# A row gradient through one DMA queue: loads and stores in threes, or in strict turn

## The chip, the cores and the metric

The kernel runs on one core of a Trainium2 chip. The metric is the device time of one execution in microseconds (us). Before the change four runs took 1247.53 to 1249.38 us, median 1249.04 us.

## What is computed

The input `x` is 8192 x 8192, float32. The output is its gradient along each row:

```
def reference(x: np.ndarray) -> np.ndarray:
    return np.gradient(x, axis=1)
```

Inside a row that is `(x[c+1] - x[c-1]) / 2`; in the first column it is `x[1] - x[0]`, in the last `x[m-1] - x[m-2]`. Every element is read once and written once: 268.44 MB in and 268.44 MB out.

## The kernel before

The 8192 rows are cut into `nsets` = 32 sets of 256 rows. Each of the 128 partitions holds R = 2 neighbouring rows of a set, so a set is 128 x 16384 float32, 8.39 MB, and a partition's part of it is one run of 65,536 bytes in memory. There are NB = 3 slots in the on-chip memory; set i lives in slot i % 3. A slot is 64 columns (SH) wider than a set: a load (L61) puts the set at column 64, and the result is written 64 columns to the left of its input in the same slot, so that a store (L97) takes columns 0 and up.

For each set there are four steps:

- L73, on POOL (GpSimd): the four end differences of each partition (two rows, two ends) go into a small tile `ends`. It waits for the set's load.
- L84, on DVE (VectorE): one custom instruction writes half the difference of the right and the left neighbour for all inner columns. It waits for L73. In the last set it is split into one instruction for each of the two rows.
- L95, a small copy that places the ends in the result, on POOL for sets with i % 5 in (1, 3), on DVE otherwise. It waits for L84.
- L97, the store, issued from SP (SyncE). It waits for L95. The last set has two stores of 4.19 MB, one for each row.

All DMAs are issued by SP, in program order, into one hardware queue (q1 in the profile). SP waits for the semaphores of a DMA before it issues it, and what comes later in SP's program waits behind. `manual_schedule` keeps the order as written, and the helper `chain` (L46 to L57) cuts each step's waits down to the ones named: a load of set i >= 3 waits only for the store of set i - 3, which frees its slot. What decides the order of the queue is where `load` is called: three loads before the loop (L67, L68), and at the end of every third turn of the loop three more (L102 to L104). With L for a load, S for a store and the set's number behind it, SP's order is

```
few L0 L1 L2 | S0 S1 S2 | L3 L4 L5 | S3 S4 S5 | L6 L7 L8 | ... | S27 S28 S29 | L30 L31 | S30 S31a S31b
```

where `few` is a load of 1 KB at L66 and S31a, S31b are the two stores of the last set.

Of the kernel before, what the change touches and what calls it, by code (L numbers as in the profile page):

```python
# [1 line left out]

# [4 lines left out]


@with_exitstack
def kernel(  # L10
    ctx: ExitStack,
    tc: tile.TileContext,
    x: bass.AP,
    out: bass.AP,
):

    nc = tc.nc
    P = nc.NUM_PARTITIONS
    n, m = x.shape
    R = 2
    NB = 3  # L30
    SH = 64  # L31
    W = R * m
    nsets = n // (P * R)
    f32 = x.dtype

    x_sets = x.rearrange("(s p t) m -> s p (t m)", p=P, t=R)
    out_sets = out.rearrange("(s p t) m -> s p (t m)", p=P, t=R)

    pool = ctx.enter_context(tc.tile_pool(name="pool", bufs=1))
    slots = [pool.tile([P, SH + W], f32, name=f"slot{k}", tag=f"slot{k}") for k in range(NB)]  # L40
    ends = pool.tile([P, nsets, R, 2], f32, name="ends", tag="ends")
    few = pool.tile([16, 16], f32, name="few", tag="few")
    loads, stores = [], [None] * nsets
    in_front = {}

    def chain(i, ins, *needed):  # L46

        group, engine = f"slot{i % NB}", ins.ins.engine  # L50
        keep = [o.ins for o in needed]
        if in_front.get(engine, (None,))[0] == group:
            keep.append(in_front[engine][1])
        tc.declare_no_dep(ins.ins, group=group, keep=keep, reason="implied by the needed step")
        tc.add_to_no_dep_group(group, ins.ins)
        in_front[engine] = group, ins.ins
        return ins  # L57

    def load(i):
        b = slots[i % NB]  # L60
        ins = nc.sync.dma_start(out=b[:, SH : SH + W], in_=x_sets[i])  # L61
        loads.append(chain(i, ins, *([stores[i - NB]] if i >= NB else [])))

    with tc.manual_schedule():

        nc.sync.dma_start(out=few[:], in_=x[0:16, 0:16])  # L66
        for i in range(NB):  # L67
            load(i)  # L68
        for i in range(nsets):
            b = slots[i % NB]  # L70
            xin = b[:, SH : SH + W].rearrange("p (t m) -> p t m", m=m)

            ins = nc.gpsimd.tensor_sub(  # L73
                out=ends[:, i, :, :],
                in0=xin[:, :, 1 : m : m - 2],
                in1=xin[:, :, 0 : m - 1 : m - 2],
            )
            at = [chain(i, ins, loads[i])]
            last = i == nsets - 1
            nr = 1 if last else R  # L80
            for r in range(0, R, nr):
                c0, c1 = r * m + 1, (r + nr) * m - 1

                ins = nc.vector._custom_dve(  # L84
                    dve_ops.TENSOR_TENSOR_REDUCE_SUB_MAX,
                    out=b[:, c0:c1],
                    in0=b[:, SH + c0 + 1 : SH + c1 + 1],
                    in1=b[:, SH + c0 - 1 : SH + c1 - 1],
                    s0=0.0,
                    s1=0.5,  # L90
                )
                halved = chain(i, ins, *at)
                res = b[:, r * m : (r + nr) * m].rearrange("p (t m) -> p t m", m=m)
                placer = nc.gpsimd if i % 5 in (1, 3) and not last else nc.vector
                ins = placer.tensor_copy(out=res[:, :, 0 : m : m - 1], in_=ends[:, i, r : r + nr, :])  # L95
                placed = chain(i, ins, halved)
                ins = nc.sync.dma_start(  # L97
                    out=out_sets[i, :, r * m : (r + nr) * m], in_=b[:, r * m : (r + nr) * m]
                )
                stores[i] = chain(i, ins, placed)  # L100
                at = [halved]
            if i % NB == NB - 1:  # L102
                for k in range(i + 1, min(i + 1 + NB, nsets)):
                    load(k)  # L104


# [1 line left out]
_INS = ['x']  # L108
_OUTS = [((8192, 8192), 'float32')]


# [23 lines left out]
```

## Time and profile before

| what | value |
|---|---|
| median of four runs | 1249.04 us |
| time of the profiled execution | 1249.38 us |
| its span, first to last instruction | 1247.4 us |
| moved | 536.88 MB, mean 430 GB/s over the span |
| DVE busy | 554.8 us (44%) |
| POOL busy | 8.9 us (1%) |
| DVE, one set (L84, 128 x 16382) | 17.22 us, 31 times |
| DVE, one row of the last set (128 x 8190) | 8.69 us, twice |
| L73 on POOL | 0.20 us, 32 times |
| L95 on DVE or POOL | 0.17 us or 0.19 us |
| load, issue to landing, median | 58.0 us |
| store, issue to landing, median | 40.4 us |

The profile of one execution gives, for each engine, its busy time; in 40 equal slices of the span the busy share of the 16 DMA engines and the GB/s that they moved; and for each group of DMA issues the time from issue to landing, which holds the time spent queued behind others. The timeline lists instructions in order of time, with the idle time of the engine ahead of them and what ended it in brackets: a POOL L73 that was released by `DMA slot<-in_x_dram` starts about 0.1 us after its load has landed, so the starts of the 32 L73 instructions are the landing times of the 32 loads. In SP's own timeline issues that follow each other are merged into one line (`x3`), with the time from the first to the last.

### The profile page before, as it was taken

Reading aid. Unit: us, or ns where it says so; the run is one execution under the profiler, and the core shown is the slowest. Engines: PE = TensorE matmul, PEld = TensorE weight load, DVE = VectorE, ACT = ScalarE, POOL = GpSimd, SP = SyncE. Lnnn points to the kernel's source line nnn. Section 1 sums busy time; section 2 is a strip of 40 time slices with the busy share of each in tenths; the row PEclk is TensorE's granted clock in tenths of the full one; section 3 lists DMA queues with packets and bytes.
Section 4 is the critical chain, followed back from the end, with each engine's and each line's share of the span. In section 5 each row is a group of like instructions: output and inputs, shape, how many; then the busy total and the mean of one; then the engine's idle time right before and its main releaser. Section 6 shows DMA issues by size and latency. Waiting matters only on the chain.

```text
span 1247.4 us, 243 instructions
## 1 busy us (share of the span) xinstructions
DVE 554.8 (44%) x54; POOL 8.9 (1%) x48
## 2 busy tenths in 40 slices
DVE  2850483069009702850582079009603840591083
POOL 0000000000000000000000000000000000000000
DMA  9999999999999999999999999999999999999989
GB/s 404 431 425 422 437 437 435 435 437 429 431 427 433 435 437 435 437 437 433 437 422 431 429 437 435 437 435 437 437 435 425 433 431 431 437 435 437 435 380 404
DMA packets 9394, 536.88 MB, mean 430 GB/s; under 512 B 1073, under 2 KB 1073, under 8 KB 1073
## 3 DMA queue, kind: packets, MB, share of 16 engines
q1 hardware_dynamic: 9392, 536.88, 99.6%
q14 instruction: 2, 0.01, 0.0%
HBM read 268.44 MB, written 268.44 MB: 430 GB/s over the span
## 4 chain that ended last, share of the span: by engine, by line
another core or an unknown queue 74%; DVE 18%; DMA 3%; issue 2%; POOL 1%; SPq 0%; POOLq 0%
DVE slot L84 18%; DMA slot<-in_x_dram 3%; POOL ends L73 0%; POOL slot L95 0%; SPq L61 0%; SPq L66 0%; DVE slot L95 0%; POOLq L130 0%
## 5 line engine op out<-in xcount | busy, mean ns | idle before, releaser
L84 DVE CUSTOM_DVE_ANT_0 slot<-slot 128x16382 f32<-128x16382 f32 (+1 forms) x33 | 551.3, 16706 | 670.2 <-POOL ends L73 670.2
L73 POOL TENSOR_TENSOR ends<-slot 128x4 f32<-128x4 f32 x32 | 6.4, 200 | 991.1 <-DMA slot<-in_x_dram 991.1
L95 DVE COPY slot<-ends 128x4 f32<-128x4 f32 (+1 forms) x21 | 3.6, 172 | 0.7
L95 POOL COPY slot<-ends 128x4 f32<-128x4 f32 x12 | 2.3, 191 | 207.9 <-DVE slot L84 207.9
L119 POOL MEMSET const-bfloat16-1.0<- 128x1 bf16 x1 | 0.1, 102 | 0.0
L119 POOL MEMSET const-uint8-127<- 128x1 uint8 x1 | 0.1, 102 | 0.0
L119 POOL MEMSET const-float32-0.0<- 128x1 f32 x1 | 0.1, 99 | 0.2 <-issue 0.2
L119 POOL MEMSET const-float32-1.0<- 128x1 f32 x1 | 0.1, 99 | 0.0
## 6 DMA issues: line engine op xcount, KB each, us to landing
out_dram<-slot SPq DMA_DIRECT2D x2, 4096.0 KB, 20.2
slot<-in_x_dram SPq DMA_DIRECT2D x32, 58.0
out_dram<-slot SPq DMA_DIRECT2D x31, 40.4
few<-in_x_dram SPq DMA_DIRECT2D x1, 1.0 KB, 1.4
```

Source lines behind the costliest of these rows:

```text
L73: ins = nc.gpsimd.tensor_sub(out=ends[:, i, :, :], in0=xin[:, :, 1 : m : m - 2], in1=xin[:, :, 0 : m - 1 : m - 2],)
L84: ins = nc.vector._custom_dve(dve_ops.TENSOR_TENSOR_REDUCE_SUB_MAX, out=b[:, c0:c1], in0=b[:, SH + c0 + 1 : SH + c1 + 1], in1=b[:, SH + c0 ...
L95: ins = placer.tensor_copy(out=res[:, :, 0 : m : m - 1], in_=ends[:, i, r : r + nr, :])
L119: nc = _bacc.Bacc("TRN2", target_bir_lowering=False, num_devices=1)
```

## The change

The loads are no longer called three at a time at the end of every third turn. From turn 1 to turn 29 each turn ends with one load, that of set i + 2. An empty line higher up goes as well.

```
@@ -99,9 +98,8 @@
                 )
                 stores[i] = chain(i, ins, placed)
                 at = [halved]
-            if i % NB == NB - 1:
-                for k in range(i + 1, min(i + 1 + NB, nsets)):
-                    load(k)
+            if 1 <= i < nsets - 2:
+                load(i + 2)
```

SP's order becomes

```
few L0 L1 L2 | S0 S1 | L3 S2 | L4 S3 | L5 S4 | L6 S5 | ... | L30 S29 | L31 S30 S31a S31b
```

The DMAs, their sizes, the slots, the arithmetic and each step's waits are the same; only the place of the loads L3 to L31 in SP's program differs. A load of set i + 2 still waits for the store of set i - 1.

## The prediction

> **What bounds the kernel now.** I read the page first: the slices and the DMA queue.
>
> ```profile
> DMA  9999999999999999999999999999999999999989
> GB/s 404 431 425 422 437 437 435 435 437 429 431 427 433 435 437 435 437 437 433 437 422 431 429 437 435 437 435 437 437 435 425 433 431 431 437 435 437 435 380 404
> q1 hardware_dynamic: 9392, 536.88, 99.6%
> L84 DVE CUSTOM_DVE_ANT_0 slot<-slot 128x16382 f32<-128x16382 f32 (+1 forms) x33 | 551.3, 16706 | 670.2 <-POOL ends L73 670.2
> ```
>
> The 16 DMA engines are busy from end to end (99.6% of the span) and DVE is idle for more than half of it. The transfers are the bound, and the only thing to win or lose is the rate at which they run. That rate has a ceiling of 437 GB/s that many slices touch and none passes; others lie at 422 to 433.
>
> Second, the timeline of POOL. Each L73 starts when its load has landed, so these starts are landing times:
>
> ```profile
> 140.69 0.20 POOL L73 TENSOR_TENSOR ends<-slot 128x4 f32<-128x4 f32 x1 [77.24 <-DMA slot<-in_x_dram]
> 160.02 0.20 POOL L73 TENSOR_TENSOR ends<-slot 128x4 f32<-128x4 f32 x1 [1.62 <-DMA slot<-in_x_dram]
> 180.11 0.20 POOL L73 TENSOR_TENSOR ends<-slot 128x4 f32<-128x4 f32 x1 [19.89 <-DMA slot<-in_x_dram]
> 257.60 0.20 POOL L73 TENSOR_TENSOR ends<-slot 128x4 f32<-128x4 f32 x1 [77.29 <-DMA slot<-in_x_dram]
> ```
>
> L4 lands 19.33 us after L3, L5 lands 20.09 us after L4. The next triples give 19.36 and 19.88, 19.34 and 19.75, 19.36 and 20.30. So the second load of a triple costs 19.33 us, which is the plain price of 8.39 MB (434 GB/s), and the third, the one with a store behind it, costs up to 1 us more. Over the ten triples the third load's surplus is 1.36 (L2), 0.76, 0.55, 0.42, 0.97, 0.01, 0.22, 0.00, 0.27, 0.28 us.
>
> Third, windows of 2.4 us around the end of L5 show where inside the load the surplus lies:
>
> ```profile
> 169.60:172.00 2.40, 2.40 (x1) 0.00 (x0) 1.00 1.01 437
> 172.00:174.40 2.40, 2.40 (x1) 0.00 (x0) 1.00 1.01 437
> 174.40:176.80 2.40, 2.40 (x1) 0.00 (x0) 1.00 1.27 437
> 176.80:179.20 2.40, 0.85 (x2) 0.00 (x0) 1.00 0.89 382
> 179.20:181.60 2.40, 1.26 (x1) 0.20 (x1) 1.00 1.01 437
> ```
>
> (The last number is GB/s, the one ahead of it the DMA share.) The rate is 437 until the last packets of L5 and 437 again with S3; it dips to 382 just at the switch from load to store. S3 had been in the queue since 158.43 and no engine ran dry, so this is no gap in the supply. At the end of L2 the same view gives 191 GB/s in one window of 2.4 us.
>
> Last, a whole cycle of three stores and three loads, from one first load to the next, lasts 116.91, 116.56, 116.41, 116.93, 116.37, 116.19, 115.92, 116.23, 116.30 us (L3 to L30), mean 116.42. Six plain transfers are 6 x 19.32 = 115.92. So one pair of switches, store to load and load to store, costs **0.50 us** on average, from 0.00 to 1.01; of that the third loads explain 3.48 / 9 = 0.39 and the other switch and rounding 0.11. In the last five cycles the mean is 0.28, in the first four 0.78.
>
> **The change part by part.** Removed and added in bytes, DMAs or instructions: nothing. Moved: 29 loads in SP's program, each with one DMA.
>
> *Does the queue run dry?* I lay the new order out with 19.32 us a transfer and 17.8 us from a landing to the store's issue (0.1 to start, L73 0.20, L84 17.22, L95 0.17 or 0.19, some 0.1 between). L2 lands at 63.2. S0 (issued at 40.88) runs to 82.5, S1 (issued at 60.30) to 101.8. L3 waits for S0: issued at 82.6, as now, runs 101.8 to 121.2. S2 is ready at 80.9 and now stands behind L3 in SP's program, so it is issued at about 83.0, 2 us later than it could be; it is not wanted until 121.2. L4 waits for S1 (101.8), runs 140.5 to 159.8. S3 is ready at 121.2 + 17.8 = 139.0 and is wanted at 159.8. L5 waits for S2 (140.5) and is wanted at 179.1. S4 is ready at 159.8 + 17.8 = 177.6 and wanted at 198.5. From there it repeats: a load is in the queue 38.6 us, a store 20.8 us before its turn, one or two transfers stand behind the running one, and SP's wait for a slot holds up no store that is needed. The compute of one set per 38.6 us stays hidden. Cost 0; if this cover were gone, each store would come with a hole (priced below).
>
> *The end.* Now S30 is issued at 1206.20, and L31 lands at 1207.8: the queue runs down, and the window 1203 to 1206 moves 66 GB/s. From L31's landing two plain transfers are 38.6, which gives 1246.4 of 1247.4: at most 1.0 us can come from that hole, and nothing if the slowest DMA engine finished L31 as S30 arrived. In the new order S30 is ready 20.8 us early. Bounds -1.0 to 0; I take 0, since the three windows around show some engines idle while others still moved L31, and the slowest decides.
>
> *The switches.* After L2, before has nine full pairs plus the switch into L30, whose other side is the run-down end. The new order has 29 pairs (S1-L3-S2 up to S29-L31-S30). The first switch, L2 to S0, is the same in both. No row shows loads and stores in strict turn, so the price of such a pair is bounded by the pairs here: 0.00 (the cycle of 115.92) and 1.01 (that of 116.93). With 4.54 us of surplus in before's nine pairs:
>
> - mean price 0.50: 29 x 0.50 - 4.54 = +10.0 us
> - first four as in before (3.13), then 25 at the late mean of 0.28 = 7.0: 10.1 - 4.54 = +5.6 us
> - at the ends: 0.00 gives -4.5, 1.01 gives +24.8
>
> The surplus shrinks in later cycles, which favours the second, but the late rows scatter (0.45, 0.27, 0.00, 0.31, 0.38) and do not go to nothing. Also the trace's DMA packet records show that by then the last engine ends a transfer over 4 us after the first, and it is the late engines that lose, because they still load while the others already store; with three times as many switches that lag has more occasions. I take the middle, 0.42 a pair: 29 x 0.42 - 4.54 = **+7.6 us**. Against the profiled execution 1249.38 + 7.6 = **1257.0 us**. That execution is 0.3 us over the median of 1249.04.
>
> A rule that would make it far worse: the Trainium skill, "DMA: Bandwidth & Descriptors", section "Anatomy of one DMA — SWDGE (gpsimd) path", puts a fixed cost of about 2.0 us on each DMA, mostly the receipt of the last write. Were that paid at every switch from load to store, 20 more of them would be 40 us by that page's figure, an estimate of 1289. The rows speak against it: 19.33 us between two landings leaves no 2 us, and a pair costs 0 to 1.01. The same page ("Two DMAs through the same engine are not ordered") says that an engine's reading and writing sides are separate and pipelined, which could let a store's reads run beside a load's writes and make switches a gain; no landing here is under 19.33 us apart, so nothing of the kind shows.
>
> **The rivals.**
>
> *Switches cost (forecast).* For: eight of ten third loads are longer than plain (by 0.22 us or more), no second load is, and the dip lies at the switch. Against: the price varies from 0 to 1.36 with no visible reason. 0.27 to 0.65 a pair: 1253 to 1264, centre 1257.
>
> *It is the third load, not the switch (faster).* The surplus could belong to three loads in a row with three stores piled up behind them, the deepest the queue gets. With one or two transfers waiting, as laid out above, the surplus would go: 1249.38 - 4.5 = 1244.8, or 1243.8 with the hole at the end. It decides from a price under 0.07 a pair (29 x 0.07 - 4.5 = -2.5). For it: cycles with 0.00 exist. Against: L2 had only S0 and just then S1 behind it, and paid the most, 1.36.
>
> *Cheap switches (same).* The engines drift apart and stop hindering each other, 0.07 to 0.24 a pair: 1247 to 1252.
>
> *Mixed traffic feeds on itself (much slower).* The lag between DMA engines grows until loads and stores always run side by side; at the early price of 0.78, 29 x 0.78 - 4.54 = +18 us, 1267; at 1.01, 1274. For it: the 191 GB/s window. Against: the trend falls.
>
> *The queue runs dry.* If my margins are wrong by a whole transfer, each set has a hole like that of 1203 to 1206, about 3 x (1 - 66/437) = 2.5 us, 29 times: 1322. The margins of 20.8 us speak against it.
>
> **How the numbers follow.** Forecast 0.60, faster 0.12, same 0.15, much slower 0.11, dry 0.02. A measurement of this kernel tells 0.2% (2.5 us) from no change, so faster is 0.12, same 0.15, slower 0.73. The range leaves out the faster case below 1247 and the part of the slow cases above 1268, some 0.20 in all: 1247 to 1268. The forecast's own range is 1253 to 1264.
>
> **What would show it.** Right: loads landing every 38.6 to 39.2 us, mean about 39.06 (2 x 19.32 + 0.42); slices mostly under 435 GB/s and none over 437; dips at the ends of loads; no window near 66 GB/s; SP issuing each store some 20 us before the load ahead of it lands. Wrong: landings every 38.64 us, or a mean rate over 430 GB/s (the third-load rival); landings over 41 us apart with idle windows (dry queue); a transfer faster than 19.32 us, which would mean that reads and writes help each other.

## The result, and the profile after

The changed kernel takes **1250.57 us** (median, 1249.10 to 1252.26), the kernel before 1248.90 us beside it: a ratio of 1.0015, 95% interval 1.001 to 1.002. I had forecast 1257.0. The direction holds, the size is a quarter of it: 1.7 us instead of 7.6, the place where my rival of cheap switches stood (1247 to 1252).

The page of the kernel after, its rate in 40 slices and its queue:

```profile
GB/s 403 436 430 411 434 436 436 434 422 436 434 432 432 422 436 430 434 436 434 434 436 424 436 436 432 434 432 426 434 436 435 432 436 432 434 434 436 436 434 342
q1 hardware_dynamic: 9392, 536.88, 99.6%
```

The queue is as full as before (99.6%) and the ceiling as high. Most low slices lie among the first 22; from the 23rd to the 39th all but one (426) are at 432 to 436. New is the last slice: 342 GB/s, where the kernel before had 404. Some DMA engines are done there while others still move data.

The timeline of POOL, the landing times of L2 to L7 and of the last three loads:

```profile
62.85 0.20 POOL L72 TENSOR_TENSOR ends<-slot 128x4 f32<-128x4 f32 x1 [2.64 <-DMA slot<-in_x_dram]
121.25 0.20 POOL L72 TENSOR_TENSOR ends<-slot 128x4 f32<-128x4 f32 x1 [58.21 <-DMA slot<-in_x_dram]
160.06 0.20 POOL L72 TENSOR_TENSOR ends<-slot 128x4 f32<-128x4 f32 x1 [21.09 <-DMA slot<-in_x_dram]
199.34 0.20 POOL L72 TENSOR_TENSOR ends<-slot 128x4 f32<-128x4 f32 x1 [39.08 <-DMA slot<-in_x_dram]
238.84 0.20 POOL L72 TENSOR_TENSOR ends<-slot 128x4 f32<-128x4 f32 x1 [39.30 <-DMA slot<-in_x_dram]
278.91 0.20 POOL L72 TENSOR_TENSOR ends<-slot 128x4 f32<-128x4 f32 x1 [22.36 <-DMA slot<-in_x_dram]
...
1132.38 0.20 POOL L72 TENSOR_TENSOR ends<-slot 128x4 f32<-128x4 f32 x1 [20.95 <-DMA slot<-in_x_dram]
1170.99 0.20 POOL L72 TENSOR_TENSOR ends<-slot 128x4 f32<-128x4 f32 x1 [38.41 <-DMA slot<-in_x_dram]
1209.65 0.20 POOL L72 TENSOR_TENSOR ends<-slot 128x4 f32<-128x4 f32 x1 [38.46 <-DMA slot<-in_x_dram]
```

From L3 on a landing follows the last by two transfers and one pair of switches; plain is 2 x 19.32 = 38.64. Early the differences are 38.81, 39.28, 39.50, 40.07 us; at the end 38.61 and 38.66. Summed: from L2 to L12 (21 transfers, 10 pairs) the surplus over plain is 4.87 us, from L12 to L22 (20, 10 pairs) it is 2.03, from L22 to L31 (18, 9 pairs) it is 0.02. So a pair costs 0.49, then 0.20, then **0.00 us**. That is nearly the whole difference from my sum: 29 pairs were to cost 29 x 0.42 = 12.2 us and cost 6.92. The early price is near the 0.42 that I had put on all of them, and it did not last. (Another 0.3 us lies at L2, whose switch I had taken to be the same in both kernels: L2 takes 20.35 us here and 20.69 before.)

Windows show it too, the first around the switch from L2 to S0, the second around the end of L27 (the last number is GB/s).

```profile
57.40:59.80 2.40, 2.40 (x1) 0.00 (x0) 1.00 1.42 437
59.80:62.20 2.40, 0.15 (x1) 0.19 (x1) 1.00 0.51 218
```

```profile
1051.80:1054.20 2.40, 0.00 (x0) 0.00 (x0) 1.00 1.01 437
1054.20:1056.60 2.40, 1.27 (x1) 0.20 (x1) 1.00 1.01 437
```

The first switch takes the rate down to 218 GB/s; the late one cannot be seen. In the trace's DMA packet records each engine carries a load as eight packets of 65,536 bytes, and a plain packet takes 2.42 us. The last packet of L2 took 3.15 to 3.70 us on all 16 engines: the surplus lies in the last packets ahead of the store.

What goes with it is in the same records, which give the end of each transfer on each of the 16 DMA engines. Worked out from them, the lag of each engine behind a schedule of 19.32 us a transfer (19.318 before rounding), in us, sorted (zero is the first engine at the end of L1):

```
after, L1    0.0  0.1  0.2  0.2  0.2  0.2  0.2  0.2  0.2  0.3  0.3  0.3  0.3  0.4  0.5  0.5
after, L7    1.8  2.0  2.1  2.1  2.1  2.2  2.5  2.5  2.9  3.1  3.1  3.2  3.3  3.5  3.6  5.1
after, L12   2.2  2.3  2.3  2.3  2.3  2.4  2.6  2.6  3.2  4.2  4.2  4.2  4.6  4.8  4.8  6.5
after, L22   2.2  2.3  2.3  2.3  2.4  2.4  2.8  3.1  5.3  6.2  6.4  6.5  6.7  6.9  7.2  8.6
after, L31   2.2  2.3  2.3  2.3  2.4  2.4  3.7  3.7  5.3  6.2  6.4  6.5  6.7  6.9  7.2  8.6
before, L31  2.4  2.4  2.4  2.5  2.6  2.7  2.8  2.9  2.9  2.9  3.0  3.1  3.3  4.9  6.2  6.9
```

In the changed kernel the engines start together and come apart into two halves of eight; the last loss of the last engine (0.5 us) is at L21, where the means of the halves are 4.0 us apart. In the kernel before thirteen engines stay within 0.9 us of each other and three fall behind. The last engine, which sets the end, has lost 8.6 us against 6.9 in the kernel before: 1.7 us, the measured difference.

### The profile page after: what moved, and what is told of

Read it like the earlier page. It is cut to its first block, busy times and chain, and to the rows that moved or that the text cites. A ratio compares the mean times of both kernels' runs of the same rounds, so it can differ in the third digit from the quotient of the medians.

```text
span 1249.2 us, 242 instructions
## 1 busy us (share of the span) xinstructions
DVE 554.8 (44%) x54; POOL 8.9 (1%) x48
## 3 DMA queue, kind: packets, MB, share of 16 engines
q1 hardware_dynamic: 9392, 536.88, 99.6%
## 4 chain that ended last, share of the span: by engine, by line
another core or an unknown queue 68%; DVE 18%; DMA 8%; issue 3%; POOL 1%; SPq 0%; POOLq 0%
DVE slot L83 18%; DMA slot<-in_x_dram 5%; DMA out_dram<-slot 3%; POOL ends L72 0%; POOL slot L94 0%; DVE slot L94 0%; SPq L65 0%; POOLq L128 0%
```

## The experiments

**Theory A** (formed on the result, "drift" in the expectations): a switch from load to store costs an engine time only while the engines run in step; each loss pushes them apart, and apart they lose nothing more. **Theory B**: the price falls with time or with the place in memory. **Theory C** (as I predicted): a switch has its price, whatever the engines do. "Surplus" below is the time from L0's landing to L31's in the profiled execution, less 61 x 19.32 = 1178.5 us. It is 6.2 us before (1207.86 - 23.19) and 8.0 after (1209.65 - 23.14).

**One switch instead of 30.** All loads, then all stores; the gradient is left out.

```
         for i in range(NB):
-            load(i)
+            nc.sync.dma_start(out=slots[i % NB][:, SH : SH + W], in_=x_sets[i])
+        for i in range(NB, nsets):
+            nc.sync.dma_start(out=slots[i % NB][:, SH : SH + W], in_=x_sets[i])
         for i in range(nsets):
+            nc.sync.dma_start(out=out_sets[i], in_=slots[i % NB][:, SH : SH + W])
```

> The same 64 transfers and the same queue with one switch only: all 32 loads, then 32 stores of what the slots hold; the gradient is left out (no L73, L84, L95), so only its time counts. If all of the surplus over plain transfers comes from switches (every theory but one), it takes what before takes less its later losses: 1248.9 - (6.9 - 2.1) = 1244, and the landings of the loads are 19.32 us apart. If something else slows the queue now and then (refresh, time), it takes 1247 to 1249 and has long landings in the middle of a run of loads.

Measured: 1243.88 us (ratio 0.9969, 0.9957 to 0.9982). The kernel before took 1247.87 us beside it and 1248.90 over all its runs, so 4 to 5 us of its time belong to the change between loads and stores, and some 6 us of the time after: that is all that an order of the queue can win. (The gradient is missing too, but it is not what costs: a run below that has it loses 1.2 us in all with 30 switches.) The last engine's lag grows here by 0.03 us a load and not at all in the stores. The one switch that is left costs nothing: L31 takes 19.35 us like the loads ahead of it, and its last packets 2.42 to 2.44 us, although the engines end it within 0.6 us of each other. So engines in step do not always lose at a switch, and Theory A as worded does not say when they do.

**The engines brought into step again, twice.**

```
-            if 1 <= i < nsets - 2:
+            if 1 <= i < nsets - 2 and i not in (11, 21):
+                if i in (12, 22):
+                    load(i + 1)
                 load(i + 2)
```

> Strict turn, but at two places (sets 12 and 22) the two loads that would follow S11 and S21 come after S12 and S22, so that the queue just runs down and the 16 DMA engines start the next store together, as at the end of the kernel before (S30). Two pairs of switches fewer, nothing else. Theory A, the drift: switches cost only while the engines run in step and push them apart until nobody hinders anybody; then each stretch of ten sets loses again what the first lost in the changed kernel (about 5 us from L3 to L10), and the time rises by 5 to 9 us, to 1256 to 1260, with the spread of the landings of one load back under 1 us after S12 and S22. Theory B, the price falls with time or with the place in memory whatever the engines do: the landings after S12 and S22 stay at 38.6 to 38.9 us and the time stays at 1250 to 1251.

Measured: 1263.27 us (ratio 1.0112, 1.0095 to 1.0129). Landings around S12, from the timeline of POOL:

```profile
473.56 0.20 POOL L72 TENSOR_TENSOR ends<-slot 128x4 f32<-128x4 f32 x1 [20.90 <-DMA slot<-in_x_dram]
533.25 0.20 POOL L72 TENSOR_TENSOR ends<-slot 128x4 f32<-128x4 f32 x1 [59.49 <-DMA slot<-in_x_dram]
552.80 0.20 POOL L72 TENSOR_TENSOR ends<-slot 128x4 f32<-128x4 f32 x1 [1.84 <-DMA slot<-in_x_dram]
595.38 0.20 POOL L72 TENSOR_TENSOR ends<-slot 128x4 f32<-128x4 f32 x1 [42.38 <-DMA slot<-in_x_dram]
634.61 0.20 POOL L72 TENSOR_TENSOR ends<-slot 128x4 f32<-128x4 f32 x1 [39.03 <-DMA slot<-in_x_dram]
```

L15 lands 42.58 us after L14, 3.9 over plain, where the changed kernel had 39.29 at the same place. The windows show that most of it is the switch from L15 to S14, which had been issued at 570.49:

```profile
590.00:592.40 2.40, 0.00 (x0) 0.00 (x0) 1.00 0.36 137
592.40:594.80 2.40, 0.00 (x0) 0.00 (x0) 1.00 0.95 410
594.80:597.20 2.40, 1.59 (x1) 0.20 (x1) 1.00 1.01 437
```

The surplus is 21.4 us, 13.4 more than in the changed kernel, with two switches fewer. By the packet records the last engine loses 3.4 us of it in the holes, where the queue had run down (S12, S13, S22, S23; S13 and S23 also came just in time, which I had not seen); the other 10 are new losses of engines that had been brought back to within 0.6 us of each other, nearly all of them at switches (0.9 us is at L13, which has a load behind it). Theory B falls: late switches are dear again, and the places in memory are the same. The size is above the 5 to 9 us that A expected.

**The matrix backwards.**

```
-        ins = nc.sync.dma_start(out=b[:, SH : SH + W], in_=x_sets[i])
+        ins = nc.sync.dma_start(out=b[:, SH : SH + W], in_=x_sets[nsets - 1 - i])
```

(and the same index in the stores).

> The sets are taken from the last rows of the matrix to the first; order of the queue as in the changed kernel. Theory A (drift): long landings early, plain ones (38.64 us) from about the 20th on, as in the changed kernel, 1250 to 1252. Theory B in its form of place in memory: plain landings in the early turns, long ones in the late turns.

Measured: 1250.84 us (ratio 1.0018, 1.0009 to 1.0028), surplus 7.9; the last engine's lag is 6.3 us at L10, 8.5 at L20 and 8.5 at L31. Place in memory is out.

**More switches, shorter packets.** Sets of one row per partition.

```
-    R = 2
-    NB = 3
+    R = 1
+    NB = 6
...
-            if 1 <= i < nsets - 2:
-                load(i + 2)
+            if 2 <= i < nsets - 4:
+                load(i + 4)
```

> Sets of one row per partition (4.19 MB, runs of 32768 bytes), six slots, six loads, three stores, then strict turn: 59 switches from load to store instead of 30. Theory A (drift, the loss is capped by how far the engines must be apart): 1249 to 1253. A fixed price per switch at the changed kernel's mean (8.55 us of lag over 30 switches, 0.24 each): 7 us more, 1257. A price in proportion to the last packet, which is half as long: 1250.

And two at a time:

```
+            if i % 2 == 1 and 3 <= i < nsets - 4:
+                load(i + 3)
+                load(i + 4)
```

> As the run with half sets in strict turn, but two loads and two stores at a time after the first six loads and four stores: 30 switches of packets of 32768 bytes, bytes per run as in the changed kernel. Price per switch independent of the packet: 1250.6, as the changed kernel. In proportion to the packet: half the loss, about 1247. Theory A (drift): between these, and the same as half sets in strict turn within 2 us.

Measured: 59 switches 1251.51 us (ratio 1.0022, 1.0013 to 1.0032); 30 switches 1253.25 us (1.0034, 1.0021 to 1.0047). Twice the switches do not cost more, if anything less, so a fixed price is out, and so is one in proportion to the packet. A holds only in part: 1251.51 lies in its range, and the two runs are within 2 us of each other, but 1253.25 lies above everything that was expected of the second run, A's share included (1247 to 1250.6). Why the fewer switches should be the dearer is not shown; the two runs' ranges overlap (1251.0 to 1253.8 and 1252.1 to 1254.3).

**Two loads and two stores in turn, full sets.**

```
-            if 1 <= i < nsets - 2:
+            if i % 2 == 1 and i < nsets - 2:
                 load(i + 2)
+                if i + 3 < nsets:
+                    load(i + 3)
```

> No lead; after L2 the queue holds two stores and two loads in turn: 16 switches from load to store, between the kernel before (11) and the changed one (30). Price per switch as I predicted (0.42 a pair): 1248.9 + 6 x 0.42 = 1251.4, more than the changed kernel's 1250.6. Loss capped by the drift: between the two, 1249 to 1250.6.

Measured: 1249.91 us (ratio 1.0010, 1.0000 to 1.0019), between the two orders, though the interval does not part it clearly from either, and below what a price of 0.42 would give. With one, 11, 16 and 30 switches the times are 1243.9, 1248.9, 1249.9 and 1250.6: the first ten beyond the one cost 4 to 5 us, the next nineteen 1.7.

**A lead for half of the engines.** Small DMAs of 8 partitions in front of L0, which only some of the engines carry:

```
         nc.sync.dma_start(out=few[:], in_=x[0:16, 0:16])
+        nc.sync.dma_start(out=slots[2][0:8, SH : SH + W], in_=x_sets[0][0:8])
```

> The changed kernel with one small DMA more at the start: 8 partitions of 65536 bytes into slot 2, which L2 overwrites. Eight partitions go to fewer than 16 engines, so some engines start the loads one packet (2.4 us) behind the others. Theory A (drift): part of the distance that the engines would have to be pushed apart is there from the start, so the later losses are smaller and the packet is paid once: 1248 to 1251, against 1250.6. Every theory in which a switch has its price whatever the distance of the engines: 1250.6 + 2.4 = 1253.

The same with a second one (`slots[2][8:16]` from `x_sets[0][8:16]`):

> As the run with one small DMA, with two of them, so that some engines start 4.8 us behind, about the distance between the two groups of engines at the end of the changed kernel (2.3 us and 5 to 8.5 us of lag). Theory A: hardly any loss after L2, the last engine ends at 0.5 + 4.8 + 1.2 = 6.5 us of lag instead of 8.55: about 1248.6. A price that does not know the distance: 1250.6 + 4.8 = 1255.4.

Measured: 1266.23 and 1262.75 us. Both forms of my expectation failed, in part since the small DMAs are slow (L0 lands at 31.75 and 40.73 instead of 23.14). What counts is the surplus after L0: 17.0 us with one, **1.3 us with two**. I tried other leads to see whether the distance or the slow start makes the difference.

```
+        nc.sync.dma_start(out=slots[2][0:128:16, SH : SH + 16384], in_=x_sets[0][0:128:16, :16384])
```

> As the runs with small DMAs at the start, but the 8 partitions lie 16 apart, so that they should not slow each other: one small DMA puts some engines one packet (2.4 us) behind. The earlier leads gave a distance of 1.9 us between two halves of the engines, with a loss of 0.6 us a switch, and of 4.0 us, with none. If the distance between the halves decides, and 2.4 is still too near: 1257 to 1262. If it is enough: 1243.9 + 2.4 = 1246.3. If a switch has a price that does not know the distance: 1253.

With a second one, from partition 1 on, of 8192 or 16384 columns:

> The same with 65536 + 32768 bytes in two small DMAs, a distance of 3.6 us. If the distance decides and its limit is under 3.6: 1243.9 + 3.6 = 1247.5 and landings every 38.64 us from the start. If the limit is higher: 1255 or more.

> The same with two small DMAs of 65536 bytes per partition, a distance of 4.8 us. If the distance decides, this is the lossless run with a cheaper start: 1243.9 + 4.8 = 1248.7, landings every 38.64 us. If the lossless run was so for another reason (its late start, its slow first packets), 1255 to 1265.

Then with neighbouring rows as the source (`x_sets[0][0:8]`, `x_sets[0][8:16]`), in the changed kernel, and last in the kernel before:

> As the lead of 3.6 us in the changed kernel, but the small DMAs read neighbouring rows of the matrix, so that the start should cost little more than the lead itself. If the distance between the two halves of the engines decides and over 3.3 us is enough: L0 to L31 in 1180 us as in the lossless run (61 plain transfers are 1178.5), total 1243.9 + 3.6 to 5 = 1248 to 1249. If the distance comes out under 3 us, losses as in the run with 2.2 to 2.8: L0 to L31 in 1186 to 1190.

> The same with two full packets, 4.8 us. If the distance decides: lossless, L0 to L31 in 1180 us, total 1249 to 1251. If the lossless runs were lossless for their slow start: L0 to L31 in 1186 or more.

> The kernel before (threes) with the same two small DMAs at the start. If the distance between the engines sets the price and the number of switches does not matter: lossless too, L0 to L31 in 1180 us instead of 1184.67, and the same time as the strict turn with the same lead within 1 us. If the number of switches matters beside the distance: 2 to 4 us less than the strict turn with the lead.

Measured, ordered by the distance between the means of the two halves at the end of L0 (packet records):

| run | distance, us | L0 lands | surplus, us | time, us |
|---|---|---|---|---|
| after, no lead | 0.2 | 23.14 | 8.0 | 1250.57 |
| strict turn, 2.4 | 1.9 | 30.03 | 7.3 | 1257.62 |
| strict turn, one | 1.9 | 31.75 | 17.0 | 1266.23 |
| strict turn, 3.6 | 2.3 | 32.61 | 10.2 | 1261.41 |
| strict turn, 3.6, other rows | 2.3 | 32.31 | 10.1 | 1262.08 |
| strict turn, 4.8 | 3.4 | 35.91 | 1.2 | 1258.03 |
| strict turn, 4.8, other rows | 3.6 | 36.14 | 1.5 | 1258.19 |
| threes, 4.8, other rows | 3.6 | 36.32 | 0.9 | 1257.83 |
| strict turn, two | 4.1 | 40.73 | 1.3 | 1262.75 |

The rate of the run at 3.4 us, from its page, and its landings (L0, L1, L2, L3 and the last two):

```profile
GB/s 284 434 434 434 434 434 434 434 434 434 434 434 434 434 434 434 434 434 434 434 434 434 434 434 434 434 434 434 434 433 434 434 434 434 434 434 434 434 434 353
```

```profile
35.91 0.20 POOL L74 TENSOR_TENSOR ends<-slot 128x4 f32<-128x4 f32 x1 [35.47 <-DMA slot<-in_x_dram]
55.24 0.20 POOL L74 TENSOR_TENSOR ends<-slot 128x4 f32<-128x4 f32 x1 [19.13 <-DMA slot<-in_x_dram]
74.68 0.20 POOL L74 TENSOR_TENSOR ends<-slot 128x4 f32<-128x4 f32 x1 [1.74 <-DMA slot<-in_x_dram]
132.45 0.20 POOL L74 TENSOR_TENSOR ends<-slot 128x4 f32<-128x4 f32 x1 [57.57 <-DMA slot<-in_x_dram]
...
1176.95 0.20 POOL L74 TENSOR_TENSOR ends<-slot 128x4 f32<-128x4 f32 x1 [38.47 <-DMA slot<-in_x_dram]
1215.63 0.20 POOL L74 TENSOR_TENSOR ends<-slot 128x4 f32<-128x4 f32 x1 [38.47 <-DMA slot<-in_x_dram]
```

434 from the second slice to the next to last, but for one of 433: 30 switches, and they cannot be seen. (The 433 goes with L24, which lands 0.6 to 0.7 us late in all four runs that hardly lose. By the packet records a packet of 8,192 bytes of the instruction queue, q14, passes in this load, at 929 us in this run, and the data packet that starts beside it takes 2.83 us instead of 2.42.) Even L2, which took 20.35 us in the changed kernel with S0 behind it, takes 19.44. In threes with the same distance it is the same, to 0.6 us: in these runs the order of the queue does not matter. All four runs from 3.4 us up lose 0.9 to 1.5 us, all five below lose 7 to 17 us. Which rows are read makes no difference, and among these four runs the start differs by 4.8 us; but all four also start later than the five others, so that a late start is not taken apart from the distance by these runs alone. The expectations named nominal leads; the distance reached is smaller, and the two runs meant as 3.6 us came out at 2.3. The totals expected of a lead that works (1248.7 and 1249 to 1251) were missed by 7 to 9 us, since the start is slow with every small DMA; what came true is L0 to L31 in 1180 us. A lead of 1.9 to 2.3 us is no step on the way: three of those four runs lose more than no lead at all. (Times are medians, the other columns are from the profiled execution.)

**Loads and stores on two queues.**

```
-                ins = nc.sync.dma_start(
+                ins = nc.scalar.dma_start(
                     out=out_sets[i, :, r * m : (r + nr) * m], in_=b[:, r * m : (r + nr) * m]
```

> Stores are issued from ScalarE's queue instead of SP's, nothing else: loads and stores are then in flight side by side on every DMA engine, a switch at every packet instead of at every transfer. Theory A in the narrow sense (only a switch of engines in step costs): the total stays at 1247 to 1254. If it is mixed traffic as such that slows a load (my rival of much slower): each of the 256 load packets of an engine loses 0.1 to 0.3 us, 1275 or more.

Measured: 1251.8 us, 1248.3 to 1264.2 (ratio 1.0045, 1.002 to 1.007). The time scatters more than with any other kernel here, and three of the ten executions lie above the 1254 that A allowed, but loads and stores side by side are not dear as such. My rival of mixed traffic that feeds on itself, 1275 or more here, is out.

## Why the forecast was too high, by its steps

- *The transfers are the bound, 19.32 us each.* Right. The run with one switch was expected at 1244 from this price and gave 1243.88.
- *The queue does not run dry.* Right. S4 was to be ready at 177.6 and L6 to follow S3's landing at about 179; SP's timeline after has

```profile
177.75 0.33 SPq L96 DMA_DIRECT2D out_dram<-slot  x1
179.54 0.34 SPq L60 DMA_DIRECT2D slot<-in_x_dram  x1
```

- *The end costs nothing.* Right as far as it can be seen: the last engine's lag does not change over S30 in either kernel.
- *The surplus belongs to the switch from load to store.* Right in the main: with one switch there is 4 to 5 us less than with 11, and the stretched packets lie at the switch. But a switch need not cost anything, as the single one shows. The rival of the third load falls, as the changed kernel, without three loads in a row, loses early at 0.49 a pair.
- *A pair costs 0.42 us on average, 29 times.* **This step failed.** It measured 6.92 / 29 = 0.24 (L2 to L31): 0.49, 0.20 and 0.00 by thirds. The 0.42 was the middle of 0.50 throughout and of a sum with 3.13 us for the first four pairs and 7.0 for the other 25; these took 2.1 and 4.8, so even the lower sum was too high. I had put 0.28 as a floor under the late pairs because the late rows of before scattered. I also had the packet records in hand and read them the wrong way round: I saw that the engines drift apart and took the drift for something that makes switches dearer. In the changed kernel it goes with cheaper ones, and two changes of the distance point the same way: the step back into line (+13.4 us of surplus) and the leads of 3.4 us and more (0.9 to 1.5 us of surplus instead of 8.0). The late rows of before (0.45 to 0.00) are cheaper than its early ones; that they too were on their way to nothing, only slowly, with a third of the switches, is not shown.
- *Cheap switches*, the rival, named this reason and a price of 0.07 to 0.24. I gave it 0.15.

What stays open: why engines in step hinder each other at a switch, why hardly at one from store to load, and why the one switch of the run without the gradient cost nothing with the engines in step. In the kernel before the late switches cost little with the halves only 1.3 to 1.6 us apart. A halfway distance is no help: at 1.9 and 2.3 us the first switches, from L2 to L3 or L5, cost nothing, then the losses set in and run to 7 to 17 us, and in those runs they went on beyond the 3.4 us that sufficed from the start. At L24 the run "strict turn, one" still lost 1.2 us, with the halves some 7 us apart. So "apart" is shown for leads of 3.4 us and more that stand from the start, all with a late start beside them; distance alone does not set the price, and the exact condition is not shown.

No version that computes the gradient beat both kernels. With a lead of about 3.4 us the losses are nearly gone, but the last engine has to be that far behind. From the time before: 1249.38, less the 4.7 us of surplus that a lead takes away (6.2 - 1.5), plus a distance of 3.5, is 1248.2, an estimate and within 0.1% of what it is; the small DMAs that made the lead brought L0 13 us later instead of 3.5.

## What to carry to other kernels

When transfers fill the span, count what a DMA queue loses against its plain rate (here 4 to 5 us of 1249) before reordering it: that is the most an order can give back. A loss that 16 parallel engines meet together need not add up per event (here 0.49 us a pair early, 0.00 late): read the price from the late events too, and look at how far apart the engines end each transfer. And a point at which the queue runs down for a moment can bring them into step again and cost far more than the hole itself (10 us against 3.4 here).

## What the runs showed that I had not expected

- In the changed kernel half of the engines fall behind the other half, and the two halves settle at some 4 us; which engines these are cannot be told from the records.
- A DMA of 8 neighbouring partitions, 65,536 bytes each, held its engines some 8 us instead of 2.42, and the other engines' first packets of L0 took about 8 us as well; spread over every 16th partition it was still 4 to 7 us. L0 landed 7 to 9 us late for one such DMA, 13 to 18 for two of full length.
- Transfers half as long, 128 loads and stores instead of 65, cost 0.9 us in all in strict turn (1251.51 against 1250.57) and 2.7 us two at a time (1253.25). The Trainium skill's fixed cost of about 2.0 us for each DMA ("DMA: Bandwidth & Descriptors", "Anatomy of one DMA — SWDGE (gpsimd) path"), given there for DMAs issued by GpSimd, does not show in this queue, which SP fills and which always holds the next one.
